# Feed-forward operands of a hybrid decoder block: tokens 0-1023 made beside mixer blocks 2 and 3 and parked in DRAM, tokens 1024-2047 made through the first down stage

## The chip, the cores and the metric

The kernel runs on one core of a Trainium2 chip. The metric is the device time of one execution in microseconds (us). Engines are named as the profile names them: PE (TensorE matmul), PEld (its weight load), DVE (VectorE), ACT (ScalarE), POOL (GpSimd), SP (SyncE, which here issues every DMA).

## What is computed

One decoder block on a float32 sequence of 2048 tokens of width 1024 (sequence 1 of 1). A mixer (attention and mLSTM side by side) adds to x; then a SwiGLU feed-forward layer of width 2816 adds to x again. The change touches the border between the two.

```python
mod = c @ w_ada + b_ada           # shift/scale/gate for the mixer and for the feed-forward layer
h = rms_norm(x, g_pre_mix) * (1 + scale_m) + shift_m
proj = h @ w_in                   # q, k, v, o and gates of both branches
...
mix = merged @ w_out
x = x + gate_m * rms_norm(mix, g_post_mix)          # called x1 below
h2 = rms_norm(x, g_pre_ffn) * (1 + scale_f) + shift_f
ff = (silu(h2 @ w_ffn_gate) * (h2 @ w_ffn_up)) @ w_ffn_down
x = x + gate_f * rms_norm(ff, g_post_ffn)
```

## The kernel before

**Precision.** Each float32 matmul is done as three float32r matmuls of a high and a low part (`mm3`, L204): hi*hi, hi*lo, lo*hi. To split an operand, ACT casts it to the high part (L259, L1112) and DVE subtracts that from the operand (L260, L1113).

**Mixer.** `block(b)` runs four times, over 512 tokens each. Its last two matmul stages are the mLSTM branch weights (`branch_tiles(w_bm, ...)`, 96 matmuls of 512 columns) and `residual_out` on w_out (192 matmuls), which writes x1 to DRAM (L541) and leaves one factor for each token in `rx`. Between pieces of matmul work, generators ("streams") are stepped: `spawn` puts a generator on a list with a due time, `tick()` after every three matmuls steps whichever is due, `finish()` runs one to its end. Time there is a count: each matmul adds a fixed price to `now[0]` (216 ns for 512 float32r columns).

**Feed-forward.** Tokens are taken 1024 at a time (`b2` = 0, 1), as a 2x2 block product with seven multiplications (Winograd's form). `gate_up(b2)` runs 11 pairs of columns, each with seven products on the gate weights and seven on the up weights, 12 matmuls a product: 1848 matmuls. `down(b2)` runs seven products over 11 steps: 924 matmuls. In `down`, products 0, 2, 4, 6 (`IN_X`) gather in the `acc` banks of PSUM, products 1, 3, 5 in the four `mix` banks, and streams are ticked only beside the former (`weave`).

**The operands in question.** The right-hand sides of `gate_up` are seven matrices, `NAMES` = 11, 21, T2, T4, T1, T3, 22, each [128, 4, 512] in a high and a low part (1 MB a part), kept in `HC`. `h_combine(b2, ...)` (L1186 on) makes them, in four rounds `k`. A round loads four pieces of x1 (L1196), multiplies by `rx` (L1205), turns each by four PE transposes (L209), scales and shifts on the way out of PSUM (L1215 on DVE, L1217 on ACT), forms T1 to T4 (L1224, L1226, L1227, L1232) and splits all seven (L1112, L1113).

For tokens 0-1023, `h_combine` is spawned in `stage5` of mixer block 3 (L1045 on), that is, ahead of the last two matmul stages of the mixer, and is finished at the end of that block. It has two of its seven results, T3 and 22, written to DRAM unsplit (`hc_d`, L1234); `rest_of_hc` (L1243 on), the first item of the feed-forward program, reads them back and splits them (L1247, L1249, L1250). For tokens 1024-2047 it is spawned at the start of `down(0)` (`next_h`), with due times 38 us of count long in all.

**Buffers and order.** SBUF is tight. `tx`, `tm` and `gg_m` belong to the mixer (`p1`); `open_ffn` closes that and opens the feed-forward pool `fpool`, whose tiles (`unit()`) lie in the same place. `big` is a ring of nine 8 KB tiles used by both. Weights go through two `raw` buffers. `run` and `run2` issue loads and splits ahead of the matmuls. In `run2` before, this began only after `open_ffn`. `build()` asks the framework to order each engine's instructions by a simulated timeline (`schedule_with_timeline_sim=True`), the program's order being the priority; so an instruction can stand earlier in the trace than in the program.

**Conditioning.** `ada_stream` computes shift, scale and gate; it is spawned in `stage6` of block 0 with a gap of 12 us for the three feed-forward parts and finished in `stage5` of block 3.

Of the kernel before, what the change touches and what calls it, by code (L numbers as in the profile page):

```python
# [19 lines left out]
P = 128  # L20
# [47 lines left out]
def decoder_block(ctx: ExitStack, tc: tile.TileContext, a: dict, out: bass.AP, dbg=None):  # L68
# [14 lines left out]
    ps_mix = ctx.enter_context(tc.tile_pool(name="ps_mix", bufs=4, space=PSUM))  # L83
    tpool = p1.enter_context(tc.tile_pool(name="tpool", bufs=1))
    mpool = p1.enter_context(tc.tile_pool(name="mpool", bufs=1))
    kvp = p1k.enter_context(tc.tile_pool(name="kvp", bufs=1, side="right"))

    uid = [0]
# [562 lines left out]
    def block(b):  # L651
# [426 lines left out]
        yield from residual_out(KD, lambda kk, t: tuple(R[m, kk // 4][:, kk % 4, t * P:(t + 1) * P] for m in ("mh", "ml")),  # L1078
                                a["w_out"][0], big, load_rows(x_d[b * TB:(b + 1) * TB, :]), gg_m, x1[b], b * NT)
        yield lambda: finish([R["hp"] if b + 1 < NBLK else R["hc"]])  # L1080

    R_ada = []

# [20 lines left out]
    def quad(t):  # L1104
        return t.rearrange("p (k c) -> p k c", k=4)
# [16 lines left out]
    def run2(items):  # L1122
        items = list(items)
        parts = [p for p in items if isinstance(p, Part)]
        raws = []
        for p in parts:
            if p.raw not in raws:
                raws.append(p.raw)
        nload = nprep = done = 0
        made = {}  # L1130

        def advance():
            nonlocal nload, nprep
            while True:
                alive = sum(1 for r in raws[max(0, nload - 3):nload] if r.left)
                if nload < len(raws) and alive < 2:
                    raws[nload].tile = raws[nload].load()
                    nload += 1
                    continue
                if nprep < len(parts) and nprep < done + parts[nprep].ahead and parts[nprep].raw.tile is not None:  # L1140
# [7 lines left out]
        advance()  # L1148
        for it in items:
            if not isinstance(it, Part):  # L1150
                it()
                continue
            advance()
            for _ in it.mms(made.pop(done)):
                if it.weave:
                    tick()
            done += 1
            advance()
# [18 lines left out]
            HC[name][i] = big([4, TB], F32R)  # L1177
        return HC[name][i]

    def four(t):  # L1180
        return [t[:, i * 4:(i + 1) * 4, :] for i in range(4)]


    HC_FROM_MIXER = (lambda: [tm([P, 4, P]) for _ in range(4)], lambda: tm([P, TB]), lambda: tx([P, TB]), (G, V))

    def h_combine(b2, rows, quarters, sums, engs):  # L1186


        wait = b2 == 0
        QUADS = ((0, 0), (0, 1), (1, 0), (1, 1))  # L1190

        def load(k):
            xk = rows()
            for j, (half, i) in enumerate(QUADS):
                c0 = (k + 4 * half) * P
                nc.sync.dma_start(xk[j], x1[b2 * 2 + i][:, c0:c0 + P].rearrange("(t p) c -> p t c", p=P))  # L1196
            return xk

        xn = load(0)
        yield 8000.0  # L1200
        for k in range(4):
            xk = xn
            for j in range(4):
                t0 = b2 * 8 + (j % 2) * 4
                engs[j % 2].tensor_tensor(xk[j], xk[j], rx[:, t0:t0 + 4].unsqueeze(2).to_broadcast([P, 4, P]), op=ALU.mult)  # L1205
            yield 3000.0
            v = {}
            for j, (half, i) in enumerate(QUADS):
                kk = k + 4 * half
                ps = mix_tile()  # L1210
                for t in range(4):
                    transpose(ps[:, t * P:(t + 1) * P], xk[j][:, t, :])
                q = quarters()
                if wait and i:
                    V.tensor_scalar(q, ps, s2[:, kk:kk + 1], sh2[:, kk:kk + 1], op0=ALU.mult, op1=ALU.add)  # L1215
                else:
                    A.activation(q, ps, AF.Identity, scale=s2[:, kk:kk + 1], bias=sh2[:, kk:kk + 1])  # L1217
                v[f"{half + 1}{i + 1}"] = q
                if i:
                    yield 1500.0  # L1220
            if k < 3:
                xn = load(k + 1)
            v["T1"] = sums()
            engs[0].tensor_tensor(v["T1"], v["12"], v["11"], op=ALU.subtract)  # L1224
            v["T2"] = sums()
            engs[0].tensor_tensor(v["T2"], v["22"], v["T1"], op=ALU.subtract)  # L1226
            engs[1].tensor_tensor(v["12"], v["22"], v["12"], op=ALU.subtract)  # L1227
            v["T3"] = v.pop("12")
            for name in NAMES:
                if name == "T4":  # L1230
                    v["T4"] = sums()
                    engs[1].tensor_tensor(v["T4"], v["21"], v["T2"], op=ALU.subtract)  # L1232
                if wait and name in ("T3", "22"):
                    nc.sync.dma_start(hc_d[:, ("T3", "22").index(name), k, :], v[name])  # L1234
                    if name == "T3":
                        A.copy(hc_part("T3", 0)[:, k, :], v[name])
                else:
                    split_unit(v[name], hc_part(name, 0)[:, k, :], hc_part(name, 1)[:, k, :])
            yield 1500.0

    hc_d = tc.dram_tile([P, 2, 4, TB], F32, name="hc_d")

    def rest_of_hc():  # L1243
        for i, name in enumerate(("T3", "22")):
            for k in range(4):
                u = unit()
                nc.sync.dma_start(u, hc_d[:, i, k, :])  # L1247
                if name == "22":
                    A.copy(hc_part("22", 0)[:, k, :], u)  # L1249
                V.tensor_tensor(hc_part(name, 1)[:, k, :], u, HC[name][0][:, k, :].bitcast(F32), op=ALU.subtract)  # L1250

    def a_operands(raw):

# [5 lines left out]
        def make(name):  # L1259
            def prep():  # L1260
                if name == "11":
                    src = q(0, 0)
                    st["S1"], st["S2"] = quad(unit()), quad(unit())
                    V.tensor_tensor(st["S1"], q(0, 1), q(1, 1), op=ALU.add)
                    V.tensor_tensor(st["S2"], st["S1"], q(0, 0), op=ALU.subtract)
                elif name == "12":
                    src = q(1, 0)
                elif name == "22":
                    src = q(1, 1)
                else:  # L1270
                    if name == "S2":
                        t = st["S2"]
# [136 lines left out]
    def down(b2):  # L1409
# [70 lines left out]

        if not last:
            def next_h():
                q4 = []

                def quarters():
                    if not q4:
                        t = big([4, TB])
                        q4.extend(t[:, i, :] for i in range(4))
                    return q4.pop()
# [24 lines left out]
        for b in range(NBLK):  # L1514
            yield from block(b)

    run(program(), {i: lambda i=i: ada_raws.update({c0: load_ada(c0, n) for c0, n, _ in ADA[ADA_AHEAD[i - 1]:ADA_AHEAD[i]]}) for i in (1, 2)})
    open_ffn()
# [7 lines left out]
    run2(program2())  # L1526


_INS = ["x", "c", "positions", "w_ada", "b_ada", "g_pre_mix", "g_post_mix", "w_in", "b_if", "conv_w", "conv_b",
# [23 lines left out]
```

## Time and profile before

| | |
|---|---|
| median of 3 runs | 2834.61 us (2832.6 to 2836.35) |
| span of the profiled execution | 2834.9 us, clock 0.985 |
| PE busy | 2726.6 us, 12654 matmuls and transposes |
| DVE, ACT, POOL busy | 1933.0, 1225.6, 259.7 us |
| DMA | 392.14 MB, mean 138 GB/s |

Matmuls of 512 columns are shown with about 0.39 us each, but are pipelined and start 0.227 us apart; so a stretch with PE at 100% is at its pace only if the number of matmuls in it is right, and the count of instructions in a stretch (x...) tells more than the busy time. Stages on the span's axis, from the trace: mixer blocks 0 to 3 up to 1492.3 us; `gate_up(0)` to 1940.0; `down(0)` to 2184.0; `gate_up(1)` to 2608; `down(1)` to the end.

### The profile page before, as it was taken

Reading aid. Unit: us, or ns where it says so; the run is one execution under the profiler, and the core shown is the slowest. Engines: PE = TensorE matmul, PEld = TensorE weight load, DVE = VectorE, ACT = ScalarE, POOL = GpSimd, SP = SyncE. Lnnn points to the kernel's source line nnn. Section 1 sums busy time; section 2 is a strip of 40 time slices with the busy share of each in tenths; the row PEclk is TensorE's granted clock in tenths of the full one; section 3 lists DMA queues with packets and bytes.
Section 4 is the critical chain, followed back from the end, with each engine's and each line's share of the span. In section 5 each row is a group of like instructions: output and inputs, shape, how many; then the busy total and the mean of one; then the engine's idle time right before and its main releaser. Section 6 shows DMA issues by size and latency. Waiting matters only on the chain. (4 is left out here: it accounts for less than half of the span.)

```text
span 2834.9 us, 35116 instructions
## 1 busy us (share of the span) xinstructions
PE 2726.6 (96%) x12654; PEld 2210.2 (78%) x12654; DVE 1933.0 (68%) x3772; ACT 1225.6 (43%) x2269; POOL 259.7 (9%) x271
## 2 busy tenths in 40 slices
PE   6999999999999999999987999999998999999997
PEld 4778887788877887778866788887777888888886
DVE  7768656586575875757676877668657676676556
ACT  4543465434644346543344333335544333333444
POOL 3100121012200112101241000000000000000000
PEclk8999999999999999999988999999999999999999
DMA  7234252243522425223347833325557333233557
GB/s 228 88 108 109 96 187 87 82 121 103 189 88 80 122 93 178 91 80 97 97 146 260 293 122 112 111 88 162 193 188 247 108 108 102 100 112 129 183 201 245
DMA packets 274774, 392.14 MB, mean 138 GB/s; under 512 B 18581, under 2 KB 175897, under 8 KB 274601
## 3 DMA queue, kind: packets, MB, share of 16 engines
q1 hardware_dynamic: 274600, 389.91, 42.2%
q8 instruction: 99, 1.62, 0.2%
q14 instruction: 75, 0.61, 0.1%
HBM read 318.52 MB, written 71.34 MB: 138 GB/s over the span
## 5 line engine op out<-in xcount | busy, mean ns | idle before, releaser
L1112 ACT CAST hl<-raw 128x512 fp32r<-128x512 f32 x528 | 314.4, 621 | 446.9 <-PE mix L204 197.8
L1113 DVE TENSOR_TENSOR hl<-raw,hl 128x512 fp32r<-128x512 f32 x528 | 352.4, 689 | 194.2 <-ACT hl L1112 191.8
L259 ACT CAST whi<-raw 128x1024 fp32r<-128x1024 f32 (+1 forms) x208 | 212.1, 1020 | 478.9 <-PE acc L204 420.4
L260 DVE TENSOR_TENSOR wlo<-raw,whi 128x1024 fp32r<-128x1024 f32 (+1 forms) x208 | 251.5, 1210 | 179.5 <-ACT whi L259 178.4
L204 PE MATMUL acc<-hhi,wlo 128*128 128x512 f32 x896 | 354.5, 396 | 0.0
L204 PE MATMUL acc<-hlo,whi 128*128 128x512 f32 x896 | 352.1, 393 | 0.0
L204 PE MATMUL acc<-hhi,whi 128*128 128x512 f32 x896 | 352.0, 393 | 0.0
L204 PE MATMUL acc<-hl,hl 128*128 128x512 f32 x1056 | 255.2, 400 | 17.9 <-DVE hl L1113 11.9
L204 PE MATMUL acc<-big,hl 128*128 128x512 f32 x1056 | 254.5, 390 | 0.0
L204 PEld LDWEIGHTS acc<-hl,hl 128*128 128x128 f32 x1056 | 200.3, 192 | 68.8 <-DVE hl L1113 19.1
L204 PEld LDWEIGHTS acc<-big,hl 128*128 128x128 f32 x1056 | 199.1, 189 | 41.6
L204 PE MATMUL mix<-big,hl 128*128 128x512 f32 x704 | 199.9, 395 | 7.2 <-DVE hl L1113 7.2
L204 PEld LDWEIGHTS acc<-hlo,whi 128*128 128x128 f32 x896 | 168.3, 188 | 41.2 <-issue 6.5
L204 PEld LDWEIGHTS acc<-hhi,whi 128*128 128x128 f32 x896 | 168.4, 188 | 39.4 <-issue 6.5
L204 PEld LDWEIGHTS acc<-hhi,wlo 128*128 128x128 f32 x896 | 168.3, 188 | 38.5 <-issue 4.1
L204 PE MATMUL mix<-hl,hl 128*128 128x512 f32 x792 | 181.4, 390 | 0.9 <-ACT hl L1112 0.9
L204 PE MATMUL acc<-whi,big 128*128 128x512 f32 x512 | 168.9, 402 | 8.6 <-DVE big L525 7.6
L204 PEld LDWEIGHTS mix<-hl,hl 128*128 128x128 f32 x792 | 148.3, 188 | 33.4 <-ACT hl L1112 2.6
L473 POOL TENSOR_TENSOR rs<-ms,nhalf 128x1 f32<-128x1 f32 (+1 forms) x40 | 30.0, 751 | 1456.7 <-DVE ms L470 1432.8
L204 PEld LDWEIGHTS mix<-big,hl 128*128 128x128 f32 x704 | 133.4, 190 | 37.1 <-DVE hl L1113 8.9
L204 PE MATMUL acc<-big,whi 128*128 128x512 f32 x512 | 158.4, 394 | 0.0
L204 PE MATMUL acc<-wlo,hhi 128*128 128x512 f32 (+1 forms) x384 | 140.0, 369 | 3.9 <-DVE wlo L260 3.1
(318 smaller groups left out, 4990.1 us busy)
## 6 DMA issues: line engine op xcount, KB each, us to landing
raw<-in_w_in_dram SPq DMA_DIRECT2D x76, 1024.0 KB, 5.0
as_d<-w SPq DMA_DIRECT2D x154, 256.0 KB, 2.1
raw<-as_d SPq DMA_DIRECT2D x70, 512.0 KB, 3.7
raw<-in_w_ffn_gate_dram SPq DMA_DIRECT2D x22, 1024.0 KB, 5.4
raw<-in_w_ffn_up_dram SPq DMA_DIRECT2D x22, 1024.0 KB, 5.1
raw<-ws_d SPq DMA_DIRECT2D x40, 512.0 KB, 4.4
tx<-in_w_ada_dram SPq DMA_DIRECT2D x64, 256.0 KB, 4.2
raw<-in_w_out_dram SPq DMA_DIRECT2D x16, 1024.0 KB, 5.7
```

What stands on the lines that cost most here:

```text
L204: T.matmul(o, lhsT=lhsT, rhs=rhs, start=start, stop=stop, skip_group_check=resumed)
L259: A.copy(hv, src)
L260: eng.tensor_tensor(lv, src, hv.bitcast(F32), op=ALU.subtract)
L473: G.tensor_tensor(r[:, :n], ms[:, :n], nhalf[:, :n], op=ALU.pow)
L1112: A.copy(v(hi), src)
L1113: V.tensor_tensor(v(lo), src, v(hi).bitcast(F32), op=ALU.subtract)
```

## The change

The feed-forward operands for tokens 0-1023 are made by a stream that starts in `stage6` of mixer block 1 and runs beside blocks 2 and 3, in 64 steps with a gap of 9.5 us of count. It works through its own small pool (`opool`: five 2 KB tiles `ob`, one 4 KB tile `os`); the SBUF for it is what `dynamic_dma_scratch_size=1024` leaves. Every result is split at once, and both parts are written to DRAM (28 writes of 512 KB). They are fetched back by 14 loads of 1 MB: seven in `stage5` of block 3, four after `stage6`, three in `rest_of_hc`. For tokens 1024-2047 the same generator runs beside `down(0)`, with a gap of 3.8 us, and splits straight into `HC`. All its DVE work is on DVE (half of the earlier mixer version's was on POOL). `ada_stream` is cut in two (scale and shift beside block 1's time with a gap of 9 us, the gate after). The first two weight splits of `gate_up(0)` are issued ahead of the last piece of w_out (`F["ahead"](2)`), and the weight sums S1 and S2 are formed in the third part instead of the first.

```diff
@@ stage5 of block b
             if b + 1 == NBLK:
-                finish(R_ada)
+                finish(R_ada[1:])
+                finish([F["hc"]])
                 open_hc()
-                R["hc"] = spawn(h_combine(0, *HC_FROM_MIXER), 3000.0)
+                for n_, i_ in (("11", 0), ("11", 1), ("21", 0), ("21", 1), ("T2", 0), ("T2", 1), ("T4", 0)):
+                    fetch(n_, i_)
@@ stage6 of block b
-                R_ada.append(spawn(ada_stream([(4, "scale"), (3, "shift"), (5, "gate")], 12000.0)))
+                R_ada.append(spawn(ada_stream([(4, "scale"), (3, "shift")], 9000.0)))
+            if b == 1:
+                finish(R_ada)
+                R_ada.append(spawn(ada_stream([(5, "gate")], 12000.0)))
+                R["hc"] = spawn(h_combine(0, STAGED, 9500.0), 20000.0)
+                F["hc"] = R["hc"]
...
+        if b + 1 == NBLK:
+            yield lambda: [fetch(n_, i_) for n_, i_ in (("T4", 1), ("T1", 0), ("T1", 1), ("T3", 0))]
...
+        yield from last[:-1]
+        if b + 1 == NBLK:
+            yield lambda: F["ahead"](2)
+        yield last[-1]
@@ h_combine
+    hc_d = tc.dram_tile([P, len(NAMES), 2, 4, TB], F32, name="hc_d")
+    def ob():
+        return opool.tile([P, TB], F32, tag="ob", name=nm("ob"), bufs=5)
+    def fetch(name, i):
+        nc.sync.dma_start(hc_part(name, i).bitcast(F32), hc_d[:, NAMES.index(name), i])
+    def h_combine(b2, staged, gap):
+        def put(name, k, v):
+            if staged:
+                t = opool.tile([P, 2, TB], F32R, tag="os", name=nm("os"), bufs=1)
+                split_unit(v, t[:, 0, :], t[:, 1, :])
+                nc.sync.dma_start(hc_d[:, NAMES.index(name), :, k, :], t.bitcast(F32))
+            else:
+                split_unit(v, hc_part(name, 0)[:, k, :], hc_part(name, 1)[:, k, :])
...
         for k in range(4):
+            q = {}
+            for half, i, name in ((0, 0, "11"), (0, 1, "12")):
+                x_ = load(k, half, i)
+                yield gap
+                scaled(x_, i)
+                yield gap
+                q[name] = turned(x_, k, half)
+                yield gap
+            t2 = ob()
+            V.tensor_tensor(t2, q["12"], q["11"], op=ALU.subtract)
+            put("11", k, q.pop("11"))
+            yield gap
+            put("T1", k, t2)
+            x_ = load(k, 1, 1)
+            yield gap
...
+            put("T4", k, t2)
+            yield gap
     def rest_of_hc():
-        for i, name in enumerate(("T3", "22")):
-            for k in range(4):
-                u = unit()
-                nc.sync.dma_start(u, hc_d[:, i, k, :])
-                if name == "22":
-                    A.copy(hc_part("22", 0)[:, k, :], u)
-                V.tensor_tensor(hc_part(name, 1)[:, k, :], u, HC[name][0][:, k, :].bitcast(F32), op=ALU.subtract)
+        for n_, i_ in (("T3", 1), ("22", 0), ("22", 1)):
+            fetch(n_, i_)
@@ next_h in down
-                F["hp"] = spawn(h_combine(b2 + 1, lambda: four(big([16, P])), quarters, unit, (V, V)))
+                F["hp"] = spawn(h_combine(b2 + 1, PLACED, 3800.0), 4000.0)
```

More of the change, by code (lines that the diff above doesn't have):

```diff
@@ L85, in decoder_block @@
     mpool = p1.enter_context(tc.tile_pool(name="mpool", bufs=1))
+    opool = ctx.enter_context(tc.tile_pool(name="opool", bufs=1, side="right"))
     kvp = p1k.enter_context(tc.tile_pool(name="kvp", bufs=1, side="right"))
@@ L1077, in block @@
         yield stage6
-        yield from residual_out(KD, lambda kk, t: tuple(R[m, kk // 4][:, kk % 4, t * P:(t + 1) * P] for m in ("mh", "ml")),
-                                a["w_out"][0], big, load_rows(x_d[b * TB:(b + 1) * TB, :]), gg_m, x1[b], b * NT)
-        yield lambda: finish([R["hp"] if b + 1 < NBLK else R["hc"]])
+        if b + 1 == NBLK:
+            yield lambda: [fetch(n_, i_) for n_, i_ in (("T4", 1), ("T1", 0), ("T1", 1), ("T3", 0))]
+        last = list(residual_out(KD, lambda kk, t: tuple(R[m, kk // 4][:, kk % 4, t * P:(t + 1) * P] for m in ("mh", "ml")),
+                                 a["w_out"][0], big, load_rows(x_d[b * TB:(b + 1) * TB, :]), gg_m, x1[b], b * NT))
+        yield from last[:-1]
+        if b + 1 == NBLK:
+            yield lambda: F["ahead"](2)
+        yield last[-1]
+        if b + 1 < NBLK:
+            yield lambda: finish([R["hp"]])
     R_ada = []
@@ L1130, in run2, with advance @@
         made = {}
-        def advance():
+        def advance(most=len(parts)):
             nonlocal nload, nprep
@@ L1139, in advance @@
                     continue
-                if nprep < len(parts) and nprep < done + parts[nprep].ahead and parts[nprep].raw.tile is not None:
+                if nprep < most and nprep < done + parts[nprep].ahead and parts[nprep].raw.tile is not None:
                     p = parts[nprep]
@@ L1146, in advance @@
                 return
-        advance()
+        yield advance
         for it in items:
@@ L1178, in hc_part @@
         return HC[name][i]
[L1180 to L1200, printed above, removed]
-        for k in range(4):
[L1202 to L1239, printed above, removed]
@@ new lines, in ob, with load, scaled, turned @@
+    def ob():
+        return opool.tile([P, TB], F32, tag="ob", name=nm("ob"), bufs=5)
+    def fetch(name, i):
+        nc.sync.dma_start(hc_part(name, i).bitcast(F32), hc_d[:, NAMES.index(name), i])
+    STAGED, PLACED = True, False
+    def h_combine(b2, staged, gap):
[6 more added lines that the diff above has]
+                split_unit(v, hc_part(name, 0)[:, k, :], hc_part(name, 1)[:, k, :])
+        def load(k, half, i):
+            t = ob()
+            c0 = (k + 4 * half) * P
+            x_ = t.rearrange("p (t c) -> p t c", t=4)
+            nc.sync.dma_start(x_, x1[b2 * 2 + i][:, c0:c0 + P].rearrange("(t p) c -> p t c", p=P))
+            return x_
+        def scaled(x_, i):
+            t0 = b2 * 8 + i * 4
+            V.tensor_tensor(x_, x_, rx[:, t0:t0 + 4].unsqueeze(2).to_broadcast([P, 4, P]), op=ALU.mult)
+        def turned(x_, k, half):
+            kk = k + 4 * half
+            ps = mix_tile()
+            for t in range(4):
+                transpose(ps[:, t * P:(t + 1) * P], x_[:, t, :])
+            q = ob()
+            A.activation(q, ps, AF.Identity, scale=s2[:, kk:kk + 1], bias=sh2[:, kk:kk + 1])
+            return q
+        for k in range(4):
+            q = {}
[13 more added lines that the diff above has]
+            yield gap
+            scaled(x_, 1)
+            yield gap
+            q["22"] = turned(x_, k, 1)
+            yield gap
+            V.tensor_tensor(t2, q["22"], t2, op=ALU.subtract)
+            V.tensor_tensor(q["12"], q["22"], q["12"], op=ALU.subtract)
+            put("T3", k, q.pop("12"))
+            yield gap
+            put("22", k, q.pop("22"))
+            x_ = load(k, 1, 0)
+            yield gap
+            scaled(x_, 0)
+            put("T2", k, t2)
+            yield gap
+            q21 = turned(x_, k, 1)
+            yield gap
+            put("21", k, q21)
+            V.tensor_tensor(t2, q21, t2, op=ALU.subtract)
+            yield gap
+            put("T4", k, t2)
+            yield gap
@@ L1271, in prep @@
                     if name == "S2":
+                        st["S1"], st["S2"] = quad(unit()), quad(unit())
+                        V.tensor_tensor(st["S1"], q(0, 1), q(1, 1), op=ALU.add)
+                        V.tensor_tensor(st["S2"], st["S1"], q(0, 0), op=ALU.subtract)
                         t = st["S2"]
@@ L1524, in program2 @@
             yield from down(b2)
-    run2(program2())
+    second = run2(program2())
+    F["ahead"] = next(second)
+    run(program(), {i: lambda i=i: ada_raws.update({c0: load_ada(c0, n) for c0, n, _ in ADA[ADA_AHEAD[i - 1]:ADA_AHEAD[i]]}) for i in (1, 2)})
+    open_ffn()
+    for _ in second:
+        pass
 _INS = ["x", "c", "positions", "w_ada", "b_ada", "g_pre_mix", "g_post_mix", "w_in", "b_if", "conv_w", "conv_b",
```

14 lines of the change are left out of this document (1 added, 13 removed).

## The prediction

> **What bounds the kernel now.** I read the page first: the engines' shares, then the slices.
>
> ```profile
> PE 2726.6 (96%) x12654; PEld 2210.2 (78%) x12654; DVE 1933.0 (68%) x3772; ACT 1225.6 (43%) x2269; POOL 259.7 (9%) x271
> PE   6999999999999999999987999999998999999997
> PEclk8999999999999999999988999999999999999999
> DMA  7234252243522425223347833325557333233557
> ```
>
> PE bounds the kernel; only its holes can be won. Besides the start they lie in slices 21 and 22 (1417 to 1559 us), where the clock row dips too, and in slice 31. So I asked for the busy time by stage: w_out of block 0, w_out and the stage before it (w_bm) of block 3, gate_up(0), its first part, down(0), gate_up(1), down(1), and the stretch in which the new stream will run.
>
> ```profile
> 351.30:396.90 45.60, 45.60 (x219) 37.63 (x218) 26.20 (x40) 28.18 (x53) 5.42 (x4) 1.00 0.44 146
> 1423.60:1492.30 68.70, 55.25 (x243) 43.90 (x243) 51.49 (x62) 30.45 (x51) 24.79 (x17) 0.88 0.43 132
> 1400.50:1423.60 23.10, 23.10 (x109) 19.10 (x108) 18.67 (x20) 12.46 (x16) 11.90 (x8) 1.00 0.48 146
> 1492.30:1940.00 447.70, 425.70 (x1852) 348.62 (x1851) 320.93 (x531) 162.54 (x295) 9.09 (x11) 0.98 0.48 161
> 1510.40:1650.00 139.60, 130.07 (x540) 104.01 (x541) 117.69 (x194) 46.84 (x83) 0.00 (x0) 0.96 0.81 275
> 1940.00:2184.00 244.00, 229.15 (x987) 183.67 (x985) 159.07 (x260) 124.24 (x233) 3.00 (x4) 0.97 0.60 201
> 2184.00:2608.00 424.00, 422.71 (x1856) 349.64 (x1857) 292.82 (x479) 152.30 (x273) 2.91 (x4) 1.00 0.33 111
> 2608.20:2823.80 215.60, 210.64 (x916) 170.89 (x915) 124.17 (x202) 101.26 (x192) 3.93 (x4) 1.00 0.62 212
> 760.00:1400.00 640.00, 630.63 (x3128) 507.99 (x3128) 426.65 (x979) 289.08 (x552) 84.61 (x80) 1.00 0.35 110
> ```
>
> Columns: length; then PE, PEld, DVE, ACT, POOL busy, each with its count; clock; DMA share; GB/s. The pace of PE comes from the chain of waits and a transposition from the timeline of PE:
>
> ```profile
> 2698.38 29.93 PE mix L204 x132
> 1969.98 1.04 PE L209 MATMUL mix<-ident,big 128*128 128x128 f32 x8
> 1970.77 1.17 PE L204 MATMUL acc<-hl,hl 128*128 128x512 f32 x4
> ```
>
> 29.93/132 = **0.2267 us** a matmul; eight transposes (two quarters) take 1970.77 - 1969.98 = 0.79 us, **0.099** each. At that pace block 3's last two stages (288 matmuls) need 65.3 us and take 91.8: 26.5 too long. Gate_up (1848) needs 419 and takes 447.7 the first time, 424.0 the second. Down (924) needs 209.5 and takes 244.0 the first time, 215.6 the second. The excess is in the two places where `h_combine` runs, and right behind the first.
>
> **The change, part by part.** Prices of its operations:
>
> ```profile
> L1205 POOL TENSOR_TENSOR tm<-tm,rx x8: 1040/1484/2032, 1386.4 to 1456.1; 128x512 f32<-128x512 f32 x8
> L1205 DVE TENSOR_TENSOR tm<-tm,rx x8: 679/680/1523, 1389.7 to 1458.6; 128x512 f32<-128x512 f32 x8
> L1217 ACT ACTIVATE tm<-mix,sh,s x8: 764/776/784, 1396.2 to 1459.0; 128x512 f32<-128x512 f32 x8
> L1113 DVE TENSOR_TENSOR hl<-raw,hl 128x512 fp32r<-128x512 f32 x528 | 352.4, 689 | 194.2 <-ACT hl L1112 191.8
> L1112 ACT CAST hl<-raw 128x512 fp32r<-128x512 f32 x528 | 314.4, 621 | 446.9 <-PE mix L204 197.8 <-PE acc L204 192.7 <-issue 24.5
> ```
>
> *1. Out of w_bm and w_out: -26.5.* DVE is 51.49 of 68.7 us busy there, many of its instructions at 1.5 instead of 0.68 us where POOL works beside them (the second row's spread). All of it leaves, 64 transposes too. Block 0's w_out, with 27 transposes and little else, takes 45.6 = 192 x 0.2267 + 27 x 0.08: no other hole is to be expected.
>
> *2. Into blocks 2 and 3: +6.3 and +4.* The 64 transposes are PE time wherever they stand: 64 x 0.099 = 6.3. DVE gets 16 scalings, 16 sums and 28 subtractions, 60 x 0.689 = 41.3 us (with 426.65 it is 73% of the 640), ACT 16 x 0.776 + 28 x 0.621 = 29.8 us (50%). That lies beside PE work; where cover fails, PE waits. PE misses 640 - 630.63 = 9.4 us there now. I take +4; between -1 (nothing but the transposes filling a hole) and +9.4 (holes doubled). The 28 writes and 16 loads go through SP, past w_in's loads: 28 x 0.5 + 16 x 0.25 = 18 MB over 640 us, 28 GB/s on top of 110. A load behind a waiting write is late by that wait, against a reserve of one raw buffer, 48 matmuls = 10.9 us; priced in the same +4. Two-input instructions of DVE stretched from 0.68 to 1.52 in the row above while POOL worked; POOL is busy 84.61 of 640 here, so 60 x 0.84 x 0.13 = 6.6 us more DVE time, which DVE's spare 27% takes. The Trainium skill says why (SBUF — State Buffer, Who interferes with whom): one port pair is shared by POOL and DVE's two-input operations, whoever comes first holds it for a whole instruction. By it the stream would interfere with all of POOL's 84.61 us at worst; the row's own spread gives the same worst case, no other sum.
>
> *3. The fetches: +5.* Eleven MB are loaded beside w_bm and w_out. What DMA can move, what it moved there, and w_out's price now:
>
> ```profile
> GB/s 0 23 377 20 377 193 256 259 75 59 223 390 406 403 397 410 410 383 400 419 406 406 406 413 419 400 328 277 177 288 288 251 333 379 398 380 395 200 374 118
> DMA packets 12522, 13.15 MB, mean 138 GB/s; under 512 B 496, under 2 KB 8688, under 8 KB 12518
> raw<-in_w_out_dram SPq DMA_DIRECT2D x16, 1024.0 KB, 5.7
> ```
>
> The first row is 1505 to 1530 us in 40 slices: some 400 GB/s at most. The second is 1400 to 1495: 13 MB. Seven MB are 18 us of that, four more 10 us. A w_out load (5.7 us) issued behind seven lands after some 24 us; it has about 22 (w_bm's 96 matmuls), less 2.3 for its split. So a wait of 0 to 4 us, and once more 0 to 4 behind the second four. I take 5; bounds 0 and 28 (all eleven MB waited for).
>
> *4. Behind w_out: 0, then -3.* PE's long wait, and what ended it on DVE:
>
> ```profile
> 1510.35 0.80 PE L204 MATMUL mix<-hcT4h,hl 128*128 128x512 f32 x1 [12.47 <-ACT hl L1112]
> 1504.61 0.75 DVE L537 SCALAR_TENSOR_TENSOR tx<-tx,rs,tx 128x512 f32<-128x512 f32 x1 [1.10 <-POOL rs L473]
> 1507.45 0.16 DVE L543 TENSOR_TENSOR sx<-sx 128x1 f32<-128x1 f32 x1 [2.10 <-ACT big L542]
> 1507.72 0.68 DVE L1264 TENSOR_TENSOR w<-raw 128x512 f32<-128x512 f32 x1
> ```
>
> Products 11 and 12 run already; the third needs S1 and S2 (L1264), whose `unit()` lies in the mixer's place and stands right behind the last tail instruction of residual_out (L543). That tail is a serial chain of DVE, POOL and ACT for four tokens' tiles, and is not touched. So `F["ahead"]` and the moved sums gain nothing: 12.5 us stay. Gone are the 8 subtractions and 4 casts of `rest_of_hc`, 8 x 0.689 = 5.5 us on a DVE that is busy 117.69 of 139.6; I take -3, bounds 0 and -5.5. The rest of that stretch is the down weights' sums (44 writes between 1521.3 and 1629.3), untouched.
>
> *5. down(0): -17 and +10.*
>
> ```profile
> 1940.05 2.30 PE L204 MATMUL acc<-hl,hl 128*128 128x512 f32 x9
> 1990.32 27.51 PE mix L204 x120
> PE acc L204 <- DVE hl L1113: 5.5, 4, 2.3
> L1196 SPq DMA_DIRECT2D big<-x x16: 370/500/893, 1625.0 to 1975.0; - x16
> L1359 SPq DMA_DIRECT2D ws_d<-big x44: 319/320/1667, 1521.3 to 1629.3; - x44
> ```
>
> Product 0 runs from 1940 to 1990.3 for 132 matmuls and 32 transposes, 29.9 + 3.2 = 33.1: 17 us of hole: the combination is packed into it, and the splits that DVE owes to PE come late (the third row). Spread thin, that goes. But the gap of 3.8 us is too long: ticks come only beside products 0, 2, 4, 6, each 132 x 0.216 = 28.5 us of count, which is 7 + 8 + 8 + 8 = 31 of 64 steps. The other 33 (rounds 2 and 3) are issued by `finish` behind all of down(0): 30 DVE instructions, 20.7 us. The last two rows show that the order may run ahead of the program: loads of x1 for down(0) stand at 1625, sums of all eleven pairs before 1630. So part of it moves into idle slots of DVE (159.07 of 244). Bounds 0 and +26 (20.7 of DVE and two landings); I take +10.
>
> *6. ada_stream:* same instructions, 0.
>
> Sum: -26.5 + 6.3 + 4 + 5 - 3 - 17 + 10 = -21.2, against the span of 2834.9 (0.3 above the runs' median of 2834.61): **2814 us**. Its own range takes half of the way to the bounds in each term, 11 us downward and 12 upward, without the far ends of 3 and 5, which are rivals B and C: 2803 to 2826.
>
> **The rivals.** Two of them need what x1's transfers take to land (here all reads and writes of it):
>
> ```profile
> DMA to landing us min/median/max: 2.0/3.2/6.9
> ```
>
> *A. The stall behind w_out goes too.* If the units get places that are free early, S1 need not follow the tail: for it, nine `tm` tiles are idle in block 3 once the combination is gone; against it, L1264 at 1507.72 follows L543 to the hair, with DVE idle before. 2814 - 12 = 2802.
> *B. Late weights.* The fetches cost up to 20 instead of 5: for it, 11 MB ahead of 1 MB loads with one spare buffer; against it, DMA is 0.43 busy there. 2829. The Trainium skill states the order that makes this one (DMA: Bandwidth & Descriptors, Queues, rings and completion order): each DMA engine takes a ring's descriptors in order, and SP's transfers share one ring an engine, so a weight load cannot pass the fetches; no row here shows the order itself.
> *C. The end of down(0), slower.* Place: between product 6 and gate_up(1). If nothing runs ahead, rounds 2 and 3 are a chain through five buffers, each round four times load 3.2, scaling 0.69, transposes 0.4, ACT 0.78: 20.3 us a round, 41 in all with PE idle. The other terms make -31.2, so it decides from 31 up; 2845. For it: `mix` banks are taken in products 1, 3, 5, and PE takes transposes only where it lacks matmuls. Against: the rows under 5.
> *D. Blocks 2 and 3 pay.* One `os` buffer: each put waits for the write before it (some 3 us), ACT and DVE stand still with what is queued behind them, PSUM evacuations. 28 x 3.2 = 90 us of such waits; if a quarter reaches PE, +22: 2836.
>
> **How the numbers follow.** My forecast 0.50, A 0.17, B 0.12, C 0.13, D 0.08. Under about 0.2% (5.7 us) a measurement of this kernel cannot tell a change. Faster: 0.50 + 0.17 + 0.04 of B = 0.71. Slower: C 0.13, 0.03 of D = 0.16. Same: the rest of B and D, 0.13. The range takes in A with its spread, B and D, and leaves out C: 2795 to 2838.
>
> **What would show it.** Block 3's w_bm and w_out at 66 to 73 us instead of 91.8, with gaps, if any, behind `raw<-in_w_out_dram`; the first put on SP soon after block 1; blocks 2 and 3 together some 10 us longer; still a gap of about 12 us behind the first 24 matmuls of gate_up(0), ended by S1's chain; down(0)'s product 0 at 30 to 33 us, and a burst of `hc` writes with a gap of some 10 us at its end. I am wrong if w_out stays at 60 or more, if block 2 or 3 grows by over 15, or if gate_up(1) starts later after down(0)'s start than the present 244 us.

## The result and the profile after

The changed kernel takes **2815.9 us** (median of 4 runs, 2814.0 to 2818.9) against 2835.5 for the kernel before (4 runs, 2832.6 to 2836.4): ratio 0.9934, 95% interval 0.992 to 0.9948. 2814 was forecast, so the sum was right. Its terms were not: several were off by 5 to 15 us, in opposite directions.

From the page of the kernel after, the busy time of each engine, then TensorE's 40 slices with the granted clock:

```profile
PE 2712.0 (96%) x12654; PEld 2206.6 (78%) x12654; DVE 1936.5 (69%) x3780; ACT 1241.2 (44%) x2278; POOL 237.0 (8%) x255
PE   6999999999999999999987999999997999999997
PEclk8999999999999999999998999999998999999999
```

There are still two dips, in the same slices as before: one in slices 21 and 22, the other in slice 31, at the end of down(0), where a 7 now stands for an 8. The stages of the kernel after, in busy time (columns as in the prediction): w_bm and w_out of block 3; a stretch behind w_out; gate_up(0); product 0 of down(0); products 1 to 5; product 6 and the start of gate_up(1); the rest of gate_up(1).

```profile
1395.80:1461.30 65.50, 65.50 (x290) 54.26 (x289) 31.32 (x38) 24.65 (x36) 11.97 (x9) 1.00 0.72 265
1466.90:1490.40 23.50, 0.01 (x1) 0.00 (x0) 11.14 (x23) 7.19 (x19) 6.16 (x8) 0.56 0.95 319
1490.40:1909.80 419.40, 415.58 (x1816) 342.38 (x1817) 302.94 (x490) 150.85 (x263) 0.00 (x0) 0.99 0.44 146
1909.80:1944.10 34.30, 33.59 (x149) 27.08 (x147) 20.72 (x33) 14.76 (x26) 0.00 (x0) 1.00 0.65 206
1944.10:2098.40 154.30, 152.86 (x677) 124.96 (x676) 87.97 (x139) 78.04 (x141) 0.00 (x0) 1.00 0.59 195
2098.40:2171.00 72.60, 51.75 (x202) 37.52 (x202) 65.11 (x121) 40.55 (x79) 9.09 (x8) 0.85 0.71 236
2171.00:2586.20 415.20, 415.20 (x1830) 343.67 (x1828) 280.67 (x452) 150.18 (x261) 0.00 (x0) 1.00 0.31 102
```

The third number of a row is PE's busy time. It is full in the first row (before: 91.8 us for the same matmuls), nothing in the second, nearly full in the third and fourth, and 20.9 us short in the sixth. Two marks from the timeline of PE cut the run into four pieces, the end of the long wait and the first matmul of down(0):

```profile
1490.42 0.80 PE L205 MATMUL acc<-hcT2h,hl 128*128 128x512 f32 x1 [23.51 <-ACT hl L1127]
...
1909.82 0.84 PE L205 MATMUL acc<-hl,hl 128*128 128x512 f32 x3
```

With the rows 1510.35 (a wait of 12.47) and 1940.05 of the kernel before, and the spans of 2834.9 and 2814.1 us:

| piece | before | after | difference | the prediction's terms |
|---|---|---|---|---|
| start to PE's wait behind w_out | 1497.9 | 1466.9 | -31.0 | -26.5 + 6.3 + 4 + 5 = -11.2 |
| the wait | 12.5 | 23.5 | **+11.0** | 0 |
| from its end to down(0) | 429.7 | 419.4 | -10.3 | -3 |
| down(0) to the end | 894.9 | 904.3 | **+9.4** | -17 + 10 = -7 |
| sum | 2834.9 | 2814.1 | -20.8 | -21.2 |

The first and third pieces came out 27 us better than the terms, the second and fourth 27 us worse. How far can such pieces be trusted? In the runs below whose edits do not touch a stretch, the first piece differs by up to some 5 us between executions, the wait by some 1, the third by some 1.5 and the fourth by some 4.

Why the wait grew is seen on VectorE. Its timeline in the kernel after (the bracket is the idle time before an instruction, and what ended it):

```profile
1471.31 0.69 DVE L1379 TENSOR_TENSOR big<-big 128x512 f32<-128x512 f32 x1 [2.21 <-DMA big<-in_w_ffn_down_dram]
...
1482.22 0.16 DVE L544 TENSOR_TENSOR sx<-sx 128x1 f32<-128x1 f32 x1 [0.85 <-ACT tx L543]
...
1486.49 0.69 DVE L1379 TENSOR_TENSOR big<-big 128x512 f32<-128x512 f32 x1 [3.92 <-DMA big<-in_w_ffn_down_dram]
...
1487.83 0.68 DVE L1295 TENSOR_TENSOR w<-raw 128x512 f32<-128x512 f32 x1
```

L544 is the last of the residual tail, L1295 is S1, L1379 is the first of the four sums of a pair's down weights. Down-weight loads and sums, which came behind S1 before, have been put into the tail by the framework's order. The last sx comes 21.1 us after w_out's last matmul (1461.08; before 15.4, 1492.05 to 1507.45). Then a sum that waits 3.9 us for its load stands ahead of S1 in VectorE's order. S1, which followed the tail to the hair before, is 5.6 us behind it.

What let these loads go ahead can be read on SP, first before, then after:

```profile
1507.54 5.47 SPq L1247 DMA_DIRECT2D w<-hc_d  x8
1513.37 1.01 SPq L1350 DMA_DIRECT2D big<-in_w_ffn_down_dram  x2
```

```profile
1461.31 0.33 SPq L1201 DMA_DIRECT2D big<-hc_d  x1
1461.74 1.21 SPq L1375 DMA_DIRECT2D big<-in_w_ffn_down_dram  x1
```

Before, the first down-weight loads stand behind the eight reads of `rest_of_hc`, into `unit()` tiles that come free with the mixer's tail. In after these reads are gone. The last fetch goes straight into a `big` tile, one of those for which the last three fetches waited until w_out's matmuls had read them (9.4 us in two waits), and the first down-weight load follows it at once. This is read from the two timelines; no run puts the reads back.

The other loss is seen in the transposes of the stream beside down(0), each row one piece of x1 (timeline of PE):

```profile
1910.50 0.60 PE L210 MATMUL mix<-ident,ob 128*128 128x128 f32 x4
1975.39 0.60 PE L210 MATMUL mix<-ident,ob 128*128 128x128 f32 x4
1981.43 0.66 PE L210 MATMUL mix<-ident,ob 128*128 128x128 f32 x4
2038.49 0.60 PE L210 MATMUL mix<-ident,ob 128*128 128x128 f32 x4
2044.43 0.60 PE L210 MATMUL mix<-ident,ob 128*128 128x128 f32 x4
2099.47 0.60 PE L210 MATMUL mix<-ident,ob 128*128 128x128 f32 x4
...
2150.97 1.09 PE L210 MATMUL mix<-ident,ob 128*128 128x128 f32 x4 [3.25 <-DVE ms L471]
2158.55 1.11 PE L210 MATMUL mix<-ident,ob 128*128 128x128 f32 x4 [1.15 <-DVE ob L1224]
2163.33 0.63 PE L210 MATMUL mix<-ident,ob 128*128 128x128 f32 x4 [0.19 <-DVE ob L1224]
2167.45 1.09 PE L210 MATMUL mix<-ident,ob 128*128 128x128 f32 x4 [0.45 <-DVE ob L1224]
```

One, two and two pieces lie beside products 0, 2 and 4 (the first of the sixteen stands at 1904.4, in the last matmuls of gate_up(0)). The other 10 of the 15 that the timeline has between 1910 and 2170 come from 2099 on, in product 6 and behind it. The first matmul of gate_up(1) stands at 2144.42, 234.6 us after down(0)'s first (before 2184.01, 244.0), but the last pieces and their splits break up its first products until 2171.

### The profile page after: what moved, and what is told of

It is laid out like the page before. It is cut to its first block, busy times and chain, and to the rows that moved or that the text cites. A ratio compares the mean times of both kernels' runs of the same rounds, so it can differ in the third digit from the quotient of the medians.

```text
span 2814.1 us, 35152 instructions
## 1 busy us (share of the span) xinstructions
PE 2712.0 (96%) x12654; PEld 2206.6 (78%) x12654; DVE 1936.5 (69%) x3780; ACT 1241.2 (44%) x2278; POOL 237.0 (8%) x255
## 5 line engine op out<-in xcount | busy, mean ns | idle before, releaser
L205 PE MATMUL acc<-hl,hl 128*128 128x512 f32 x1056 | 249.7, 394 | 12.9 <-DVE hl L1128 10.9
L205 PE MATMUL acc<-whi,hhi 128*128 128x512 f32 (+1 forms) x384 | 131.4, 369 | 12.7 <-ACT hhi L506 6.3
```

The costliest lines, as they stand in the source:

```text
L205: T.matmul(o, lhsT=lhsT, rhs=rhs, start=start, stop=stop, skip_group_check=resumed)
```

## The experiments

Three theories were put to the chip. **Place and queue**: S1 is late because its tile lies where the mixer's tail lay, and because down-weight work stands ahead of it. **Burst**: the steps of the stream that do not fit beside down(0) cost some 25 us at its end. **Holes**: the stream beside the mixer falls into holes of PE. Ratios are to the kernel before, timed in the same batch (2834.2 to 2835.5 us); all edits are against the kernel after. The last two columns are from the profiled execution.

| run | median us | ratio (95%) | wait behind w_out | down(0) to the end |
|---|---|---|---|---|
| after | 2815.9 | 0.9934 (0.992-0.9948) | 23.5 | 904.3 |
| e1_gap17 | 2800.6 | 0.9879 (0.9866-0.9893) | 23.7 | 886.3 |
| e2_s_ob | 2803.0 | 0.9889 (0.9875-0.9902) | 9.5 | 903.1 |
| e3_hold | 2810.3 | 0.9912 (0.9899-0.9925) | 15.2 | 904.1 |
| e4_old_down | 2814.0 | 0.9929 (0.9916-0.9942) | 23.3 | 897.1 |
| e5_all3 | 2775.4 | 0.9791 (0.9776-0.9807) | 2.0 + 1.8 | 886.4 |
| e6_gap12 | 2799.4 | 0.9866 (0.9848-0.9885) | 24.1 | 885.7 |
| e7_double | 2844.5 | 1.0031 (1.0018-1.0044) | 27.0 | 906.1 |
| e8_noahead | 2823.6 | 0.9958 (0.9944-0.9972) | 24.1 | 906.8 |
| e9_nocall | 2817.5 | 0.9939 (0.9925-0.9953) | 24.8 | 905.9 |
| e10_fetch2 | 2821.8 | 0.9957 (0.9943-0.9971) | 24.6 | 906.8 |

### e1 and e6: a closer stream beside down(0)

```diff
-                F["hp"] = spawn(h_combine(b2 + 1, PLACED, 3800.0), 4000.0)
+                F["hp"] = spawn(h_combine(b2 + 1, PLACED, 1700.0), 4000.0)
```

> One number is changed against the kernel after: the gap between the steps of the stream in down(0), 3.8 to 1.7 us. 64 steps then take 109 of the 114 us of count that products 0, 2, 4 and 6 give, so nothing is left for finish. Theory of the burst: the 33 steps that come at the end cost some 25 us of the 676.6 us from the first matmul of down(0) to the last of gate_up(1). Then this stretch falls to 648-656 and the whole from 2815.9 to 2788-2796. Rival, VectorE owes: whoever packs the steps closer makes the splits of the products late, as in product 0 of the kernel before, where four rounds cost 17 us; then the stretch stays at 666-670 and the whole is 2805-2810. Second rival, there is no price of the burst and the time is lost elsewhere (gate_up(1)'s own start): no change, 2814-2818.

Down(0) to the end is 18.0 us shorter (904.3 to 886.3), where 21 to 29 were expected for this stretch; the whole is 15.3 shorter, because what lies ahead of down(0) ended 5.1 us later in this execution. The stretch is what the edit touches. Its PE timeline, down(0)'s first matmul, the fourth piece of the stream, and the last of all:

```profile
1914.89 0.84 PE L205 MATMUL acc<-hl,hl 128*128 128x512 f32 x3
...
1926.23 0.63 PE L210 MATMUL mix<-ident,ob 128*128 128x128 f32 x4 [0.62 <-DVE ob L1224]
...
2134.09 0.60 PE L210 MATMUL mix<-ident,ob 128*128 128x128 f32 x4
```

Four pieces now stand beside each of the products 0, 2, 4 and 6 (the first at 1909.4, just ahead of product 0), none behind. VectorE owes next to nothing for it: PE waits 0.62 us ahead of the fourth piece, so that rival falls. Some hole stays at the end, as the row of e1's stretch shows (75 us, PE busy 66.42):

```profile
2100.00:2175.00 75.00, 66.42 (x284) 52.18 (x283) 62.97 (x117) 37.69 (x77) 9.31 (x8) 0.98 0.72 242
```

e6 asks whether these 8.6 us are the stream's; its only edit is 1250.0 in the same place.

> As e1 but with a gap of 1.25 us: 64 steps take 80 us of count, so the stream runs in products 0, 2 and 4 and none of it in product 6, where the first results of down(0) are finished on VectorE and PE still misses some 8 us in e1. Theory that the stream and the results' finish fight for VectorE at the end: 2-5 us less than e1, stretch 653-656, whole 2795-2799. Rival, VectorE owes again in product 0 (six rounds of four steps packed into 28.5 us): holes of 5-10 us there, stretch 660-668, whole 2802-2810. If the 8 us at the end belong to the finish alone: like e1 within 2 us.

The same stretch of e6:

```profile
2099.00:2174.00 75.00, 67.68 (x278) 53.69 (x277) 56.38 (x105) 31.92 (x67) 6.04 (x8) 0.95 0.69 233
```

Down(0) to the end takes 885.7 us against 886.3, the whole 2799.4 against 2800.6: no difference. The last piece of the stream is turned at 2075.3, and the hole at the end is still 7.3 us, so it is not the stream's. The kernel before has the same waits at this place (2.21, 2.06 and 1.28 us, from 2150 to 2186; here 2.20, 2.00 and 1.28): they belong to the end of down(0) itself. Of the 18 us that e1 won, 20.9 - 8.6 = 12.3 are holes of PE at down(0)'s end. Some 4 more, by estimate, are the clock: in that stretch of after 202 matmuls take 51.75 us of busy time, 0.256 each, at a granted clock of 0.85; in e1's 284 take 66.42, 0.234 each, at 0.98.

### e4: half of the change

The tokens 0-1023 staged as in after, those of 1024-2047 by the old `h_combine`, spawned by the old `next_h`.

```diff
+    def h_combine_old(b2, rows, quarters, sums, engs):
...
-                F["hp"] = spawn(h_combine(b2 + 1, PLACED, 3800.0), 4000.0)
+                F["hp"] = spawn(h_combine_old(b2 + 1, lambda: four(big([16, P])), quarters, unit, (V, V)))
```

> Half of the change: the operands of tokens 0-1023 are made beside the mixer and staged as in the kernel after, those of 1024-2047 by the kernel before's combination, packed into product 0 of down(0). From the stages of the two traces: the stretch from down(0)'s first matmul to gate_up(1)'s last is 668 with the old combination and 676.6 with the new, so the half alone is faster than the whole change: 2805-2809. By the prediction's step 5 (new one better by 7): 2821-2825. Product 0 of down(0) at 48-52 us again, and no gaps at down(0)'s end.

```profile
1490.48 0.79 PE L205 MATMUL acc<-hcT2h,hl 128*128 128x512 f32 x1 [23.29 <-ACT hl L1127]
...
1914.66 2.30 PE L205 MATMUL acc<-hl,hl 128*128 128x512 f32 x9
```

Down(0) to the end is 7.1 us shorter with the old combination (897.1), as the two traces said, but the whole misses the expected 2805-2809. From the end of the wait to down(0) it takes 424.2 us instead of 419.4: the old stream's first loads (1574.0) and scalings (1577.4) stand inside gate_up(0) already, as its loads did before. So the spread half of the change costs 2 us by the medians, which is within what can be told from nothing, and its gain stands in gate_up(0), where it was not looked for.

### e2 and e3: place or queue

e2 gives another place to S1, S2 and the three sums of the first gate pair.

```diff
-                        st["S1"], st["S2"] = quad(unit()), quad(unit())
+                        st["S1"], st["S2"] = quad(new()), quad(new())
...
-                combine(i, ps, R, unit, done)
+                combine(i, ps, R, new, done)
...
-            gp, up = list(pair_parts(wg, p, done_g)), list(pair_parts(wu, p, done_u))
+            gp, up = list(pair_parts(wg, p, done_g, ob if b2 + p == 0 else unit)), list(pair_parts(wu, p, done_u, unit))
```

> Against the kernel after only the place of five tiles is changed: S1, S2 and the three sums of the first pair of gate_up(0) lie in the five ob buffers, which are idle then, and not in the pool that takes the mixer's memory. Theory of the place: S1 is late because its tile's memory comes free with the last tail instruction of w_out; with another place S1 and S2 are made beside w_out, the third product starts at once, and the stall of 23.5 us behind w_out falls under 6: whole 2796-2800. Rival, the next link: gate tiles, the rest of the operands or the last fetches lie behind the same tail, the stall is only moved one product on, and the first pair of gate_up(0) gets shorter by less than 8: whole 2808-2815.

Timeline of PE, then of VectorE:

```profile
1494.71 0.79 PE L205 MATMUL acc<-hcT2h,hl 128*128 128x512 f32 x1 [9.46 <-ACT hl L1127]
...
1896.57 0.84 PE L205 MATMUL acc<-hl,hl 128*128 128x512 f32 x3
```

```profile
1446.56 0.69 DVE L1295 TENSOR_TENSOR ob<-raw 128x512 f32<-128x512 f32 x1 [4.84 <-DMA raw<-in_w_ffn_gate_dram]
...
1489.58 0.69 DVE L1379 TENSOR_TENSOR big<-big 128x512 f32<-128x512 f32 x1 [3.29 <-DMA big<-in_w_ffn_down_dram]
...
1490.92 0.68 DVE L1295 TENSOR_TENSOR w<-raw 128x512 f32<-128x512 f32 x1
```

S1 is made at 1446.6, beside w_out, 41 us earlier than in after, and PE goes on through the whole of the first gate pair. Then the same wait stands one matrix further on: the up weights' S1 lies in the old place, and the same down-weight sum stands ahead of it. Down(0) starts 13.3 us earlier (1896.57 against 1909.82). That the place makes S1 late is shown. The whole, 2803.0, lies between the two forecasts: the wait is not under 6 us, and the rival "next link" is right about where the rest stays, not about its size.

e3 leaves S1 where it is and holds back the first three down-weight loads, sums and writes.

```diff
             st["raw"] = big([2, D])
+            if p < 3:
+                V.tensor_copy(st["raw"][:, 0, 0:1], F["S1"])
             nc.sync.dma_start(st["raw"], wdn[p * 256:(p + 1) * 256, :].rearrange("(k p) c -> p k c", p=P))
...
                         V.tensor_tensor(st["S2"], st["S1"], q(0, 0), op=ALU.subtract)
+                        F.setdefault("S1", st["S1"][:, 0, 0:1])
```

> Against the kernel after one element of the tiles of the first three down-weight loads is written from S1 before the load, so that these loads, their sums on VectorE and their writes come behind S1; S1 stays where it is. Theory of the queue: the loads, sums and writes that run ahead make the tail of w_out longer (21 instead of 15 us) and stand ahead of S1 on VectorE (5 us); without them the stall falls from 23.5 to 12-14, what the kernel before had: whole 2804-2808. Rival, the fetches: the tail is long because its loads and writes share the DMA engines with the staged operands; then S1 follows the tail's last instruction, only the 5 us go: stall 17-19, whole 2810-2812. Second rival: what is held back is late later: no change or more, 2815-2820.

```profile
1479.12 0.16 DVE L544 TENSOR_TENSOR sx<-sx 128x1 f32<-128x1 f32 x1 [2.10 <-ACT big L543]
1479.38 0.68 DVE L1295 TENSOR_TENSOR w<-raw 128x512 f32<-128x512 f32 x1
```

S1 again follows the tail to the hair, and the wait is 15.2 us, 8.4 less than in after. Where 12 to 14 were expected for the queue alone and 17 to 19 for fetches alone, the wait lies between, nearer the queue (the whole, 2810.3, lies in the range given for the fetches): of the 11 us by which the wait grew, 8.4 are the down-weight work, and some 3 stay. They are the tail's: 18.6 us from w_out's last matmul (1460.52) to the last sx, 15.4 in before; its loads of x share the transfers' time with the staged operands, but no run takes the fetches away, so that last cause is argued, not shown.

### e5: the three edits together

The edits of e1 and e2, and e3's with the copy from the first S1 in the old place (that of the up weights); each pair's down-weight load stands behind its gate products.

> Three edits together against the kernel after: the gap of 1.7 us (e1), the first pair's sums in the idle ob buffers (e2), and the first three down-weight loads held back, here until the first S1 that lies in the mixer's old place, which is that of the up weights. e1 shortened the stretch from down(0) to the end of gate_up(1) from 676.3 to 658.3, e2 left a second stall of 9.5 us in front of the up weights' S2, whose S1 stood on VectorE behind a down-weight sum that waited 3.3 us for its load. If the two theories (place and queue) hold together, S1 of the up weights follows the tail's last instruction, at about 1485, and the second stall falls to 3-5 us: 2814.1 - 18 - 13 - 5 = 2776 to 2782 whole. Rival, the tail itself: the last residual loads and writes end no earlier, and DMA does the held-back loads at a worse time: the second stall stays at 8-10, whole 2783-2788. Rival, the gains overlap: above 2790.

```profile
1488.87 0.50 PE L205 MATMUL mix<-hcT4h,hl 128*128 128x512 f32 x1 [2.04 <-ACT hl L1127]
1491.44 1.22 PE L205 MATMUL mix<-hcT4h,hl 128*128 128x512 f32 x2 [1.83 <-DVE hl L1128]
...
1892.25 0.84 PE L205 MATMUL acc<-hl,hl 128*128 128x512 f32 x3
```

**2775.4 us**, 2.1% less than the kernel before and 40 less than the change. The gains add: down(0) starts 17.6 us earlier than in after, the rest is 17.9 shorter, together the 35.5 by which the spans differ (2814.1 and 2778.6). By the medians e1, e2 and e3 won 15.3, 12.9 and 5.6 us alone, 33.8 in all, and the three together 40.5.

### e7: the stream beside the mixer done twice

```diff
-        for k in range(4):
+        for k in ((0, 0, 1, 1, 2, 2, 3, 3) if staged else range(4)):
...
-                R["hc"] = spawn(h_combine(0, STAGED, 9500.0), 20000.0)
+                R["hc"] = spawn(h_combine(0, STAGED, 4600.0), 35000.0)
```

> Every step of the stream beside the mixer is done twice (same loads, scalings, transposes, sums, splits and writes, the second overwriting the first with the same data), with a gap of 4.6 instead of 9.5 us. This adds 64 transposes, 60 VectorE and 44 ScalarE instructions, 28 writes of 0.5 MB and 16 loads to blocks 2 and 3 and nothing elsewhere. By the prediction's second step a stream costs 6.3 us of transposes and 4 of cover: whole 8-12 us more than after, 2824-2828, block 2 and block 3 each 4-6 us longer. Theory from the trace of after (both blocks were no longer than before): the transposes and the rest fall into holes of PE, 0-3 us more: 2816-2819. Rival, one os buffer (D): puts twice as close behind each other now wait for writes and hold up PSUM evacuations: 15 us and more, over 2830.

The first x1 write of a block's tail on SP, in blocks 1 and 2, marks the ends of these blocks. Before, after, e7:

```profile
755.89 1.48 SPq L541 DMA_DIRECT2D x<-tx  x2
...
1114.81 1.49 SPq L541 DMA_DIRECT2D x<-tx  x2
```

```profile
753.56 1.48 SPq L542 DMA_DIRECT2D x<-tx  x2
...
1110.96 1.48 SPq L542 DMA_DIRECT2D x<-tx  x2
```

```profile
757.22 0.80 SPq L542 DMA_DIRECT2D x<-tx  x2
...
1125.64 0.80 SPq L542 DMA_DIRECT2D x<-tx  x2
```

Block 2 takes 358.9 us before, 357.4 with one stream and 368.4 with two. (e1 and e3, whose matmuls up to block 3 stand in the same order as in after, end block 1 at 757.9 and 753.3, so block 1's 2.3 us are within what executions differ by; the length of block 2 is 355.3 to 358.0 in the nine other runs with one stream.) One stream costs nothing that can be seen in block 2: PE's idle time there falls from 5.6 to 3.2 us. `ada_stream`, which the change moves too, runs in the same blocks and is not separated from it. The second stream costs 11 us in that block. The whole grew by 28.6 us, more than any theory but D's gave. ACT waited 44.3 us in all for writes out of `os` (14.7 in after), which is D's mechanism, while no wait of PE in block 2 is longer than 2.0 us; how much of the 11 us are these waits and how much the added work is not shown. Nor did the stream end in time: its last `os` write is at 1455.9, inside w_out (1385.4 in after). W_bm and w_out take 71 us instead of 65.5, and the wait behind w_out, ended by a write of down-weight sums, is 27.0 us.

### e8 and e9: the call ahead, and the place of the sums in the program

e9 leaves out the call; e8 does so too, and makes S1 and S2 with the first operand again.

```diff
-        if b + 1 == NBLK:
-            yield lambda: F["ahead"](2)
...
                 if name == "11":
                     src = q(0, 0)
+                    st["S1"], st["S2"] = quad(unit()), quad(unit())
+                    V.tensor_tensor(st["S1"], q(0, 1), q(1, 1), op=ALU.add)
+                    V.tensor_tensor(st["S2"], st["S1"], q(0, 0), op=ALU.subtract)
...
```

> Two edits of the change undone: the call that lets gate_up(0)'s first loads and splits be put ahead of the last group of w_out is left out, and S1 and S2 are made with the first operand again instead of with the third. The prediction took both at nothing: 2814-2818, the stall behind w_out at 22-25 us, ended by the same splits. Rival: without them the gate weights' first load and the first two operands come behind the tail, so products 0 and 1 of the first pair no longer run right behind w_out: the stall grows by up to 5.4 us (24 matmuls): 2819-2822.

> Only the call that puts gate_up(0)'s first loads and two operands ahead of w_out's last group is left out; S1 and S2 stay with the third operand. e8, with both edits undone, took 7.7 us more than the kernel after, with the stall unchanged (24.1) and 4 us more waiting for VectorE in gate_up(0). Theory that the place of the sums matters (S1 and S2 made later leave VectorE's turn to the splits that PE waits for): the call is worth nothing, 2814-2818. Theory that the call matters (the first raw tile of gate_up(0) is taken earlier, so everything behind it is prepared earlier): as e8, 2821-2825.

e9 is within 2 us of after: the call is worth nothing that can be measured. e8 is 7.7 us slower than after and 6.1 slower than e9, with the wait behind w_out no longer; from its end to down(0) it takes 425.5 us (1489.64 to 1915.11) instead of 419.4. What VectorE waited for in gate_up(0) (total, times, longest), the row of the down-weight loads in after, e8 and e9:

```profile
DVE big L1379 <- DMA big<-in_w_ffn_down_dram: 5.4, 3, 2.0
```

```profile
DVE big L1377 <- DMA big<-in_w_ffn_down_dram: 14.1, 4, 5.8
```

```profile
DVE big L1377 <- DMA big<-in_w_ffn_down_dram: 3.8, 3, 1.7
```

Neither expectation of e8 held whole: the wait behind w_out stayed, as the first said, and the time was lost further on. That the place of S1 and S2 in the program is worth some 6 us is shown. The rows suggest how: the program's order is the priority by which the framework orders VectorE, and with the old place VectorE stands 8.7 us longer in front of loads that have not landed, with splits for PE behind them. In the kernel before this row is 9.1 us.

### e10: the fetches twice

```diff
                     fetch(n_, i_)
+                    fetch(n_, i_)
```

and the same for the four of the second place.

> Each of the first eleven fetches of staged operands is issued twice, so that 22 instead of 11 MB are read beside w_bm and w_out. In after, these eleven cost PE nothing there (65.5 us for 65.3 at PE's pace, the weights of w_out landed in 5.0 us each). Forecast of the prediction's step 3 (weights queue behind the fetches): seven fetches more ahead of w_out's first load are some 18 us of DMA, its reserve was 22: 0 to 10 us of holes in w_bm and w_out, and the four more behind them come out of the reserve of the second half, 5 us; 2816-2830. Rival, w_out stays untouched and the operands themselves come too late for gate_up(0): w_bm and w_out at 65-66 us, the stall behind it longer by 5-15: 2820-2830. If the DMA has room for both: 2814-2818.

The traces give the landing of one of w_out's four loads, the last: 5.0 us after its issue in after, 14.3 in e10. So the doubled fetches push this load back by 9.3 us, and PE still waits only 1.7 us in w_out (0.50, 0.29 and 0.87 us, the longest at 1432.99). 2821.8 is 5.9 us over after, and PE's long wait ends 5.9 us later (1496.32), its length 1.0 more; the remainder lies in the mixer, within what executions differ by. The forecast of 0 to 10 us for w_bm and w_out holds at its low end: weights do come late behind fetches, as in rival B, at a size that this change does not reach.

## Why the prediction was right, and where it was wrong

**1. Out of w_bm and w_out, -26.5: right.** 65.5 us for 65.3 at PE's pace.

**2. Into blocks 2 and 3, +6.3 and +4: mis-sized.** "The 64 transposes are PE time wherever they stand" is the step that failed. Block 2 became no longer (357.4 for 358.9) with the stream beside it, and PE's idle time there fell by 2.4 us: what was added went in part into holes that were there. The bound of -1 ("nothing but the transposes filling a hole") was the near one. In e7 the second helping costs 11 us in block 2 alone.

**3. The fetches, +5: mis-sized, 0.** PE has no hole in w_bm and w_out. Even where the last load takes 14.3 us (e10) PE waits 1.7 us, so the reserve was larger than the sum allowed.

**4. Behind w_out, 0 and -3: both wrong.** That S1's place makes it late was right (e2); that the tail "is not touched" was not. Down-weight work came into the tail and ahead of S1: +11, of which e3 takes 8.4 back. The prediction had quoted the sums as running ahead, between 1521.3 and 1629.3, and called them "untouched": it did not ask what they would do when the reads ahead of them on SP were gone. "`F["ahead"]` and the moved sums gain nothing" holds for the call (e9) and fails for the sums (e8 against e9, 6.1 us). With the 4.8 us of the old stream's prelude (e4) these add up to the -10.3 in gate_up(0), where -3 stood for the subtractions of `rest_of_hc`; nothing to be seen is left for them, though no run tests them alone.

**5. Down(0), -17 and +10: the first right, the second mis-sized.** Product 0 takes 34.3 us instead of 50.3. Its reading was a little off: twelve matmuls of gate_up(0) (2.7 us) stand in the same stretch in both kernels, so the hole before was 14.5 us and not 17; of the 16 us won, some 2.8 are 28 transposes that went elsewhere. The burst costs 25 (9.4 + 16), near the upper bound of 26. The step that failed is "part of it moves into idle slots of DVE": ten of sixteen pieces stood at the end. e1 removes 18 of the 25. The sign of being wrong that was named for this place, gate_up(1) starting more than 244 us after down(0), did not show it: gate_up(1) started after 234.6 us and lost the time in its first products.

**6. `ada_stream`, 0:** not tested alone; nothing in the traces stands against it.

**The rivals.** A, B, C and D each named a mechanism that the runs can produce: A in e2 and e5, B in e10, C at 25 of its 41 us in after itself (not for its ground that PE takes transposes only where it lacks matmuls: in e1 all sixteen pieces stand beside matmuls), D in e7 as 44.3 us of ACT's waits, with an unknown share of PE's loss. For B, the Trainium skill (DMA: Bandwidth & Descriptors, Queues, rings and completion order) has each DMA engine take the descriptors of a ring in order; 14.3 against 5.0 us fits that, but transfers filled 97% of DMA's time from 1395 to 1445 us of e10, and sharing that time would look the same. The forecast was near by luck: terms 2, 3 and the -3 were too dear by about as much as the wait in term 4 and the burst were too cheap.

## What to carry to other kernels

Work removed from a stage lets other work forward, and what the order puts there may wait for a transfer in front of the one instruction that counts; ask of each piece removed what stood behind it, and where that will stand on its engine. A stream that is stepped by a count should be checked by division (steps times gap against the count of the stages that tick): here the steps that did not fit took 15 us by the medians (e1), where the whole change won 20. A sum that comes out right is no proof of its terms: here the errors were 27 us each way, and the two that were losses were worth 40 us to mend.

## What the runs showed of the hardware

In this wait the clock follows within 3 us. Granted clock (the third number from the end) in short stretches of the kernel after around the long wait:

```profile
1467.00:1475.00 8.00, 0.00 (x0) 0.00 (x0) 4.00 (x8) 2.47 (x7) 3.02 (x4) 0.67 0.93 316
1475.00:1483.00 8.00, 0.00 (x0) 0.00 (x0) 3.27 (x9) 3.97 (x10) 2.85 (x5) 0.50 0.98 302
...
1490.40:1493.00 2.60, 2.58 (x6) 2.00 (x7) 2.60 (x5) 2.07 (x4) 0.00 (x0) 0.50 0.95 367
1493.00:1496.00 3.00, 3.00 (x13) 2.40 (x13) 3.00 (x6) 0.15 (x1) 0.00 (x0) 0.91 0.31 117
```

0.67 over the first 8 us is full clock for some 2.7 us and half after that; behind the wait six matmuls take 2.6 us, 0.43 each for 0.2267, and the clock is full again by about 1493.5, some 3.1 us after work began. So this wait costs some 1.5 us more than its length. The Trainium skill (TensorE: Matmul & The Clock Gate, What's actually happening) gives about 3.4 us for either change; the trace's 2.8 us (from 1466.9) and 3.1 us are a little shorter.
